# A decoder trunk on one core: one more gate/up unit ahead of the token-major key units, and a last output tile split over two PSUM banks

## The chip, the core and the metric

The kernel runs on one core of a Trainium2 chip. The metric is the device time of one execution in microseconds (us), lower is better. The engines are PE (TensorE, matmuls), DVE (VectorE), ACT (ScalarE), POOL (GpSimd) and SP (SyncE, whose queue issues nearly all transfers here). Each engine works through its own list of instructions in order, and waits on semaphores for the others.

## What is computed

The reference is a small decoder trunk with 256 tokens, width 1024 and two layers. Each layer is a half-step SwiGLU feed-forward block, a mixer, and a second half-step SwiGLU block. Layer 0 mixes by a gated short convolution, layer 1 by sparse attention. Between the layers a shared set of keys and values is built.

```python
def _swiglu(x, w_gate_up, w_down):
    a, b = jnp.split(x @ w_gate_up, 2, axis=-1)
    return (jax.nn.silu(a) * b) @ w_down

h = x
for layer in range(DEPTH):                      # DEPTH = 2, D_MODEL = 1024, D_FF = 2816, SEQ = 256
    h = h + 0.5 * _swiglu(_rmsnorm(h, ffn_norm[layer, 0]), ffn_w_gate_up[layer, 0], ffn_w_down[layer, 0])
    hn = _rmsnorm(h, mix_norm[layer])
    if layer < N_A_LAYERS:
        h = h + _short_conv(hn, conv_w_in[layer], conv_w[layer], conv_w_out[layer])
    else:
        h = h + _nsa(hn, nsa_w_qg[i], q_norm[i], nsa_w_o[i], *shared)
    h = h + 0.5 * _swiglu(_rmsnorm(h, ffn_norm[layer, 1]), ffn_w_gate_up[layer, 1], ffn_w_down[layer, 1])
    if layer == N_A_LAYERS - 1:
        shared = _shared_kv(h, kv_norm, kv_w, cmp_pos, cmp_w1, cmp_b1, cmp_w2, k_norm)
return h
```

Inside `_shared_kv`, two slots of keys and values are kept raw (they are compressed by a small network later), and four are used token by token.

## The kernel before

**Arithmetic.** Every fp32 product is made from two parts: a weight tile `raw` is loaded by SP, ACT casts it to a high part `whi` (two casts of 128x1024), and DVE subtracts that from `raw` to make the low part `wlo` (two subtractions of 128x1024). Activations have a high and a low part as well. Three products are then added in PSUM: high by high, high by low, low by high.

**Units.** The program is a list of units. A unit is one weight tile with the matmuls that use it (`mm`) and what follows them (`post`). The load of a unit's weights is issued three units ahead, its split into `whi` and `wlo` is put two units ahead (`wsplit`, `LOOK`). `at_mid(u, i, f)` hangs a piece of work `f` into unit u after its i-th step. `run_units` writes all of this as one list of operations, and `Plan.schedule` reorders it with a cost model into one fixed list per engine.

**The feed-forward block and the key units.** `ffn` makes 22 gate/up units (`gate_up(ft)`, written g0, g1, ... below), then 16 down units (`down(dt, c)`: output tile dt, half c of the inner dimension). In the third block, `between(ft)` puts the units of the shared keys and values ahead of `gate_up(ft)`, by the table `KVAT`. They are `r0`, `r1` (`rawslot`: the raw slots), `t00`, `t01`, `t10`, `t11` (`tokmajor`: keys and values token by token, two units each for one result), `c00` to `c11` (`compress`) and pieces of side work. Before the change, PE's list runs r0, g0, r1, g1, t00, t01, g2, c00, g3, c01, g4, and so on.

**PSUM.** The result of a gate/up, raw or token-major unit is a pair of banks from `two_banks()`, a pool (`psA`, tile name `pa`) with two such pairs, handed out in turn. t00 and t01 share one pair. A unit may only start when the last reader of the pair's tile before is done. The readers: after a gate/up unit ACT copies half of it (`t<-pa`) and DVE adds the other half (`t<-pa,t`); after a raw unit DVE makes eight `rt<-pa,R` multiplications. For each raw unit POOL then adds positions in two operations (`rf<-rt`), ACT casts the two results and DVE subtracts (`r<-rf`, names r00, r01, r10, r11).

**Two ways to multiply.** `halves_mm` needs two matmuls for a step of 128 rows of the inner dimension, one of 512 columns (high and low activations side by side) and one of 256, and leaves two sums in the two halves of a bank, which must be added at the end. `feature_mm` needs three matmuls of 256 columns and leaves a single sum in half a bank.

**The output.** In the last block `residual` makes each output tile from a bank with two sums: two DVE operations (`scalar_tensor_tensor`, the second reads what the first wrote) and a transfer to HBM.

Of the kernel before, what the change touches and what calls it, by code (L numbers as in the profile page):

```python
# [11 lines left out]
F32 = mybir.dt.float32  # L12
# [3 lines left out]
ALU = mybir.AluOpType  # L16
# [4 lines left out]
T = 256  # L21
DT = D // 128
NF = 2816 // 128
HALF = NF // 2
# [15 lines left out]
CQ, CO, PQ, PO = 0, 0, 4, 6  # L40
YP = 1
SB, PB, FB = 4, 4, 0
KVAT = {0: [("r0",)], 1: [("r1",)], 2: [("t00",), ("t01",)], 3: [("c00",)], 4: [("c01", (4, "k0"), (7, "k1"))],
        5: [("t10", (4, "h0")), ("t11",)], 6: [("c10", (3, "sk"), (7, "sl"))], 7: [("c11",), ("", (3, "h1"), (9, "sv"))]}
HEADP = set()
WARMUP = 9
HEAD = [("h", 0, 1), (0, 0, 2), (0, 2, 4), ("h", 1, 2), (0, 4, 8), ("h", 2, 3), (0, 8, 12), ("h", 3, 4), (0, 12, 16),
# [385 lines left out]
def program(plan, a, out, ones):  # L433
    pe, ac, ve, gp, sp = (Engine(plan, k, None) for k in ("pe", "act", "dve", "gp", "sp"))
# [4 lines left out]
    work = plan.pool("work", 2)  # L439
    psB = plan.pool("psB", 2, psum=True)  # L440
    psC = plan.pool("psC", 2, psum=True)
# [13 lines left out]
    def two_banks():  # L455
        return wide["pool"].tile([128, 2, 512], F32, name="pa")

    def tt(eng, o, x, y, op):
        eng.tensor_tensor(o, x, y, op)

    def split(hi, lo, src):
        ac.copy(hi, src)
        tt(ve, lo, src, hi.bitcast(F32), ALU.subtract)

    def mm3(o, lh, ll, rh, rl, start, stop):
        pe.matmul(o, lh, rh, start=start, stop=False)
        pe.matmul(o, lh, rl, start=False, stop=False)
        pe.matmul(o, ll, rh, start=False, stop=stop)
# [3 lines left out]
    h = px[:, NPAR:].rearrange("p (a b) -> p a b", b=T)  # L472
# [17 lines left out]
    def unit(src, n, mm, post=None):  # L490
        units.append((src, n, mm, post))
        return len(units) - 1
# [61 lines left out]
    def at_mid(u, i, f):  # L554
        mid.setdefault(u, []).append((i, f))
# [67 lines left out]
    def residual(dt, ps, factor, key, gains):  # L623
        a, b = ps[:, :T], ps[:, T:]
        if gains is None:
            o = work.tile([128, T], F32, name="s1")
            ve.scalar_tensor_tensor(o, a, factor, h[:, dt], op0=ALU.mult, op1=ALU.add)
            ve.scalar_tensor_tensor(o, b, factor, o, op0=ALU.mult, op1=ALU.add)
            sp.dma_start(out[dt * 128:(dt + 1) * 128, :], o)
            return  # L630
        if dt == 0:
            NORM[key] = new_norm(gains)
        ve.scalar_tensor_tensor(h[:, dt], a, factor, h[:, dt], op0=ALU.mult, op1=ALU.add)
        ve.scalar_tensor_tensor(h[:, dt], b, factor, h[:, dt], op0=ALU.mult, op1=ALU.add)
        norm_tile(NORM[key], dt)

    def feature_mm(ps, w, kt0, x, start, stop):

        wh, wl = w
        n = wh.shape[1] // 128  # L640
        for kt in range(n):
            s = slice(kt * 128, (kt + 1) * 128)
            mm3(ps, wh[:, s], wl[:, s], x[:, kt0 + kt, 0], x[:, kt0 + kt, 1], start and kt == 0, stop and kt == n - 1)
            yield

    def halves_mm(ps, w, kt0, x, start, stop):

        wh, wl = w
        n = wh.shape[1] // 128
        for kt in range(n):  # L650
            s = slice(kt * 128, (kt + 1) * 128)
            pe.matmul(ps, wh[:, s], x[:, kt0 + kt].rearrange("p x t -> p (x t)"), start=start and kt == 0, stop=False)
            pe.matmul(ps[:, T:], wl[:, s], x[:, kt0 + kt, 0], start=False, stop=stop and kt == n - 1)
            yield

    def halves_sum(o, x, y):
        ac.copy(o, y)
        tt(ve, o, x, o, ALU.add)


    def ffn(lf, nkey, gname, okey, ogains, pool_open, between=None):
        st = {}
        fin = {}

        def spare(ft):
            return (nkey, ft) in (("n0", 2), ("n5", 0))

        def gate_up(ft):
            paired = nkey == "n0" and ft < 2

            def mm_pair(wh, wl):
                xs = NORM[nkey].sets[gname]
                if ft == 0:
                    for i in range(2):
                        ps = two_banks()
                        st["ps", i] = [ps] + [ps[:, ab] for ab in range(2)]
                pq = [st["ps", x // 2][x % 2 - 2] for x in range(4)]
                w = [[(y[:, (4 * k + x) * 128:(4 * k + x + 1) * 128]) for y in (wh, wl)] for k in range(4) for x in range(4)]
                for k in range(4):
                    kt = 4 * ft + k  # L680
                    if kt == 0:
                        for x in range(4):
                            pe.matmul(pq[x][:, :T], w[x][0], xs[:, 0, 0], start=True, stop=False)
                        for x in range(4):
                            pe.matmul(pq[x][:, T:], w[x][1], xs[:, 0, 0], start=False, stop=False)
                        for x in range(4):
                            pe.matmul(pq[x][:, T:], w[x][0], xs[:, 0, 1], start=False, stop=False)
                            yield
                        continue
                    for x in range(4):  # L690
                        yield from halves_mm(pq[x], w[4 * k + x], kt, xs, False, kt == DT - 1)

            def mm(wh, wl):
                xs = NORM[nkey].sets[gname]
                if spare(ft):
                    ps = [psB.tile([128, 512], F32, name="pb") for _ in range(2)]
                else:
                    ps = two_banks()
                    ps = [ps] + [ps[:, ab] for ab in range(2)]
                st["ps", ft] = ps  # L700
                for kt in range(DT):
                    for ab in range(2):
                        s = slice((2 * kt + ab) * 128, (2 * kt + ab + 1) * 128)
                        yield from halves_mm(ps[ab - 2], (wh[:, s], wl[:, s]), kt, xs, kt == 0, kt == DT - 1)

            def post():
                ps = st.pop(("ps", ft))
                t = work.tile([128, 2, T], F32, name="t2")
                R = NORM[nkey].R
                if spare(ft):  # L710
                    for ab in range(2):
                        halves_sum(t[:, ab], ps[ab][:, :T], ps[ab][:, T:])
                else:
                    halves_sum(t, ps[0][:, :, :T], ps[0][:, :, T:])
                tt(ve, t, t, R[:, None, :].to_broadcast([128, 2, T]), ALU.mult)
                s = work.tile([128, T], F32, name="s1")
                ac.activation(s, t[:, 0], AF.Silu)
                g = work.tile([128, T], F32, name="g1")
                tt(gp, g, s, t[:, 1], ALU.mult)
                st["g", ft] = g  # L720

            def fin_():
                if ft % HALF == 0:
                    st["gg", ft // HALF] = pool_open(st, ft // HALF).tile([128, HALF, 2, T], F32R, name=f"gg{ft // HALF}")
                g = st["gg", ft // HALF][:, ft % HALF]
                split(g[:, 0], g[:, 1], st.pop(("g", ft)))
            if paired:
                held.append((post, fin_))
                return unit(a["wgu"][lf * NF + ft], 2048, mm_pair)
            u = unit(a["wgu"][lf * NF + ft], 2048, mm, post)  # L730
            at_mid(u + 1, 1, fin_)
            return u

        def down(dt, c):
            def mm(wh, wl):
                if c == 0:
                    st["pd"] = psB.tile([128, 512], F32, name="pb")
                yield from halves_mm(st["pd"], (wh[:, :HALF * 128], wl[:, :HALF * 128]), 0,
                                      st["gg", c], c == 0, c == 1)

            def post():
                if c == 1:
                    residual(dt, st["pd"], 0.5, okey, ogains)
            return unit(a["wdn"][lf, dt, c], HALF * 128, mm, post)

        u0 = len(units)
        for ft in range(NF):
            if between is not None:
                between(ft)
            gate_up(ft)  # L750
        for dt in range(DT):
            for c in range(2):
                down(dt, c)
        return u0
# [106 lines left out]
    def shared_kv(nkey, gname):  # L861
# [210 lines left out]
        def between(ft):  # L1072
            for name, *hooks in KVAT.get(ft, []):
                u = make[name]() if name else len(units)
# [386 lines left out]
    for u, x, y in HEAD:  # L1461
        if u == "h":
            x, y = NPAR * (x > 0) + x * T, NPAR + y * T
# [142 lines left out]
```

## Time and profile before

| | us |
|---|---|
| median of three runs (lowest, highest) | 993.74 (993.33, 993.93) |
| the profiled execution's own time | 990.6 |
| its span, from the first to the last instruction | 988.8 |
| PE busy | 978.0 (99%) |
| DVE busy | 732.6 (74%) |
| ACT busy | 584.4 (59%) |
| POOL busy | 201.6 (20%) |

The span is 1.8 us shorter than the execution, and the execution 3.1 us shorter than the median of the runs. PE is busy nearly all the time, but matmuls are pipelined, so its busy time says less than the distance from the start of one to the start of the next: in a gate/up unit a pair of 512 and 256 columns starts every 0.35 us. Small pauses of PE are spread over the attention part; in the feed-forward blocks there are few.

### The profile page before, as it was taken

How to read it: one execution, taken by the hardware profiler on the slowest of the kernel's cores; microseconds unless marked ns; L12 is line 12 of the kernel's file. 1: busy time of each engine (PE TensorE's matmuls, PEld its weight loads, DVE VectorE, ACT ScalarE, POOL GpSimd, SP SyncE). 2: the span in 40 equal slices, each digit the busy share in tenths (PEclk: the TensorE clock that was granted, in tenths of full speed). 3: DMA queues.
4: the chain of work that ended last, by engine and by line, in shares of the span. 5: the costliest groups of instructions: out<-in, count | busy, mean ns of one | idle time of the engine just before them, and what ended most of it. 6: DMA issues, size and time to landing. Idle time of an engine off the chain costs nothing.

```text
span 988.8 us, 15226 instructions
## 1 busy us (share of the span) xinstructions
PE 978.0 (99%) x5792; PEld 857.7 (87%) x5792; DVE 732.6 (74%) x1087; ACT 584.4 (59%) x1047; POOL 201.6 (20%) x263
## 2 busy tenths in 40 slices
PE   9999999999999999999999999999999999999998
PEld 6888888888888888888888888888988988888887
DVE  7876666689796767677889986666778897676553
ACT  7655645555466565555478656554599775656441
POOL 2211111122221111111340111111378421111100
PEclk9999999999999999999999999999999999999999
DMA  8655445655646454456466655355510345555353
GB/s 298 236 199 175 168 149 200 203 163 193 239 172 212 172 204 152 159 193 230 179 211 215 221 210 196 127 196 176 228 66 1 117 153 201 205 178 170 125 192 109
DMA packets 30889, 177.83 MB, mean 180 GB/s; under 512 B 3424, under 2 KB 5472, under 8 KB 15968
## 3 DMA queue, kind: packets, MB, share of 16 engines
q1 hardware_dynamic: 30816, 176.86, 52.1%
q8 instruction: 45, 0.74, 0.3%
q14 instruction: 28, 0.23, 0.1%
HBM read 175.80 MB, written 1.05 MB: 179 GB/s over the span
## 4 chain that ended last, share of the span: by engine, by line
PE 87%; ACT 5%; DVE 4%; issue 2%; DMA 1%; POOL 1%; SPq 0%; POOLq 0%; DVEq 0%; ACTq 0%
PE pa L420 53%; PE pb L420 29%; PE S L420 3%; ACT P L420 3%; PE pc L420 2%; DVE wlo L420 1%; DMA raw<-in_wgu_dram 1%; ACT ph L420 1%; DVE hg L420 1%; ACT whi L420 1%; DVE px L420 0%; DVE s L420 0%; ACT qs L420 0%; DVE r L420 0%; POOL rf L420 0%
## 5 line engine op out<-in xcount | busy, mean ns | idle before, releaser
L420 PE MATMUL pa<-hg,whi 128*128 128x512 f32 (+1 forms) x1572 | 538.4, 389 | 1.4 <-ACT whi L420 1.0
L420 DVE TENSOR_TENSOR wlo<-raw,whi 128x1024 fp32r<-128x1024 f32 (+3 forms) x382 | 415.5, 1103 | 149.6 <-ACT whi L420 147.6
L420 ACT CAST whi<-raw 128x1024 fp32r<-128x1024 f32 (+3 forms) x386 | 350.7, 931 | 204.8 <-issue 83.0
L420 PE MATMUL pa<-hg,wlo 128*128 128x256 f32 x1536 | 429.8, 280 | 0.6 <-DVE wlo L420 0.6
L420 PEld LDWEIGHTS pa<-hg,whi 128*128 128x128 f32 x1572 | 292.1, 188 | 66.0 <-ACT whi L420 2.0
L420 PEld LDWEIGHTS pa<-hg,wlo 128*128 128x128 f32 x1536 | 289.9, 189 | 2.5 <-DVE wlo L420 2.0
L420 PE MATMUL pb<-gg,whi 128*128 128x512 f32 x704 | 245.0, 393 | 0.0
L420 PE MATMUL pb<-gg,wlo 128*128 128x256 f32 x704 | 195.9, 279 | 0.0
L420 PEld LDWEIGHTS pb<-gg,whi 128*128 128x128 f32 x704 | 131.8, 187 | 30.1
L420 POOL TENSOR_TENSOR g<-s,t 128x256 f32<-128x256 f32 x88 | 70.6, 803 | 421.8 <-ACT s L420 415.7
L420 PEld LDWEIGHTS pb<-gg,wlo 128*128 128x128 f32 x704 | 132.6, 188 | 0.3
L420 ACT ACTIVATE s<-t 128x256 f32<-128x256 f32 x88 | 36.8, 418 | 130.8 <-DVE t L420 130.8
L420 POOL TENSOR_TENSOR acc<-acc,sq 128x256 f32<-128x256 f32 x36 | 32.7, 907 | 179.8 <-ACT sq L420 179.3
L420 DVE TENSOR_TENSOR t<-t,R 128x512 f32<-128x512 f32 x96 | 65.7, 685 | 0.1
L420 DVE TENSOR_TENSOR t<-pa,t 128x512 f32<-128x512 f32 x94 | 64.2, 684 | 1.8 <-ACT t L420 1.7
L420 ACT COPY t<-pa 128x512 f32<-128x512 f32 x94 | 54.1, 577 | 1.1 <-PE pa L420 1.1
L420 DVE SCALAR_TENSOR_TENSOR px<-pb,px 128x256 f32<-128x256 f32 x56 | 23.7, 424 | 34.4 <-PE pb L420 33.6
L420 PE MATMUL S<-hg,whi 128*128 128x256 f32 (+1 forms) x224 | 48.7, 301 | 0.0
L420 PE MATMUL pb<-hg,whi 128*128 128x512 f32 (+1 forms) x144 | 47.9, 384 | 0.2 <-DVE hg L420 0.2
L420 DVE TENSOR_TENSOR gg<-g,gg 128x256 fp32r<-128x256 f32 x88 | 39.2, 446 | 10.7 <-ACT gg L420 10.7
L420 ACT CAST gg<-g 128x256 fp32r<-128x256 f32 x88 | 35.3, 402 | 11.7 <-POOL g L420 11.6
L420 DVE SCALAR_TENSOR_TENSOR hg<-px,hg 128x256 fp32r<-128x256 f32 x56 | 39.3, 716 | 0.2
(178 smaller groups left out, 864.1 us busy)
## 6 DMA issues: line engine op xcount, KB each, us to landing
raw<-in_wgu_dram SPq DMA_DIRECT2D x86, 1024.0 KB, 4.8
raw<-in_wdn_dram SPq DMA_DIRECT2D x64, 704.0 KB, 4.1
raw<-in_wci_dram SPq DMA_DIRECT2D x8, 1024.0 KB, 5.0
raw<-in_wci_dram SPq DMA_DIRECT2D x8, 512.0 KB, 3.6
raw<-in_wco_dram SPq DMA_DIRECT2D x4, 1024.0 KB, 4.8
raw<-in_wkt_dram SPq DMA_DIRECT2D x4, 1024.0 KB, 4.9
raw<-in_wc_dram SPq DMA_DIRECT2D x4, 1024.0 KB, 4.8
raw<-in_wq_dram SPq DMA_DIRECT2D x4, 1024.0 KB, 4.9
```

Source lines behind the costliest of these rows:

```text
L420: getattr(engines[op.eng], op.name)(*[real(x) for x in op.args], **{k: real(v) for k, v in op.kw.items()})
```

## The change

The first part is in the table `KVAT`: from t00 on, each entry moves to the next `ft`, so that g2 comes ahead of t00 and every later key unit comes one gate/up unit later. The second is in `down`: for the last output tile of the last block (dt = 7) the two halves c = 0 and c = 1 no longer add into one bank. Half 0 goes into a bank of its own by `halves_mm`, and after it two DVE operations add it to `h`. Half 1 goes into half a bank of the pool `psC` by `feature_mm`, and one DVE operation makes the output from it and `h`.

```diff
-KVAT = {0: [("r0",)], 1: [("r1",)], 2: [("t00",), ("t01",)], 3: [("c00",)], 4: [("c01", (4, "k0"), (7, "k1"))],
-        5: [("t10", (4, "h0")), ("t11",)], 6: [("c10", (3, "sk"), (7, "sl"))], 7: [("c11",), ("", (3, "h1"), (9, "sv"))]}
+KVAT = {0: [("r0",)], 1: [("r1",)], 3: [("t00",), ("t01",)], 4: [("c00",)], 5: [("c01", (4, "k0"), (7, "k1"))],
+        6: [("t10", (4, "h0")), ("t11",)], 7: [("c10", (3, "sk"), (7, "sl"))], 8: [("c11",), ("", (3, "h1"), (9, "sv"))]}
...
         def down(dt, c):
             def mm(wh, wl):
+                if dt == DT - 1 and ogains is None:
+                    ps = (psC if c else psB).tile([128, 512], F32, name="pc" if c else "pb")
+                    st["pd", c] = ps
+                    if c == 0:
+                        yield from halves_mm(ps, (wh[:, :HALF * 128], wl[:, :HALF * 128]), 0, st["gg", c], True, True)
+                    else:
+                        yield from feature_mm(ps[:, :T], (wh[:, :HALF * 128], wl[:, :HALF * 128]), 0, st["gg", c], True, True)
+                    return
                 if c == 0:
                     st["pd"] = psB.tile([128, 512], F32, name="pb")
...
             def post():
+                if dt == DT - 1 and ogains is None:
+                    if c == 0:
+                        for x in (st["pd", 0][:, :T], st["pd", 0][:, T:]):
+                            ve.scalar_tensor_tensor(h[:, dt], x, 0.5, h[:, dt], op0=ALU.mult, op1=ALU.add)
+                        return
+                    o = work.tile([128, T], F32, name="s1")
+                    ve.scalar_tensor_tensor(o, st["pd", 1][:, :T], 0.5, h[:, dt], op0=ALU.mult, op1=ALU.add)
+                    sp.dma_start(out[dt * 128:(dt + 1) * 128, :], o)
+                    return
                 if c == 1:
                     residual(dt, st["pd"], 0.5, okey, ogains)
```

Outside the key part of the third block and the last tile, the lists of PE are the same. The first place is PE from the end of r1 on, before the change. `pa_4633` is the bank pair of r1, `pa_4715` that of g1, `pa_4775` that of t00 and t01, `pa_4852` that of g2. Weights stand on the left in t00 and t01, activations (`hg`) in the others.

```order
L420 MATMUL pa_4633<-hg_4024,wlo_4521 128x256
L420 MATMUL pa_4715<-hg_4029,whi_4596 128x512 [waits DVE_49]
...
L420 MATMUL pa_4715<-hg_4029,wlo_4617 128x256
L420 MATMUL pa_4775<-whi_4651,hg_4024 128x512 [waits DVE_49,PE_49,Activation_49]
...
L420 MATMUL pa_4775<-wlo_4740,hg_4024 128x512
L420 MATMUL pa_4775<-whi_4717,hg_4024 128x512
L420 MATMUL pa_4852<-hg_4029,whi_4778 128x512 [waits DVE_49]
```

The same stretch of PE after the change, where `pa_4775` is the pair of g2 and `pa_4824` that of t00 and t01.

```order
L420 MATMUL pa_4633<-hg_4024,wlo_4521 128x256
L420 MATMUL pa_4715<-hg_4029,whi_4596 128x512 [waits DVE_49]
...
L420 MATMUL pa_4715<-hg_4029,wlo_4617 128x256
L420 MATMUL pa_4775<-hg_4029,whi_4651 128x512 [waits DVE_49,PE_49,Activation_49]
...
L420 MATMUL pa_4775<-hg_4029,wlo_4674 128x256
L420 MATMUL pa_4824<-whi_4717,hg_4024 128x512 [waits DVE_49]
L420 MATMUL pa_4824<-wlo_4740,hg_4024 128x512
```

g2 now takes the pair that r1 had, and t00 the pair that g1 had. The second place is DVE from the readers of r1's pair on, after the change; before the change the same operations stand there in the same order, with other weights behind the names `wlo`. `t2_4787<-pa_4715` is the last reader of g1's pair, `t2_4834<-pa_4775` that of g2's.

```order
L420 TENSOR_TENSOR rt_4655<-pa_4633,R_4591 64x128 x8
L420 TENSOR_TENSOR wlo_4740<-raw_4549,whi_4717 128x1024 x2
L420 TENSOR_TENSOR gg0_4701<-g1_4686,gg0_4701 128x256
L420 TENSOR_TENSOR r10_4756<-rf0_4743,r10_4756 128x8x64
L420 TENSOR_TENSOR r11_4771<-rf1_4753,r11_4771 128x8x64
L420 TENSOR_TENSOR wlo_4790<-raw_4648,whi_4778 128x1024
L420 TENSOR_TENSOR t2_4787<-pa_4715,t2_4787 128x512
L420 TENSOR_TENSOR wlo_4790<-raw_4648,whi_4778 128x1024
L420 TENSOR_TENSOR t2_4787<-t2_4787,R_4591 128x512
L420 TENSOR_TENSOR wlo_4837<-raw_4713,whi_4826 128x1024
L420 TENSOR_TENSOR t2_4834<-pa_4775,t2_4834 128x512
```

Up to the second `wlo_4790` nothing moved on DVE; what moved is the unit on PE that these operations release. The third place is the end of DVE's list (before with -, after with +), where `s` is the output tile and `px` holds `h`.

```order
 L420 SCALAR_TENSOR_TENSOR s_9840<-pb,s_9840 128x256
 L420 TENSOR_TENSOR wlo<-raw,whi 128x704 x2
-L420 SCALAR_TENSOR_TENSOR s_9893<-pb,px 128x256
-L420 SCALAR_TENSOR_TENSOR s_9893<-pb,s_9893 128x256
+L420 SCALAR_TENSOR_TENSOR px<-pb,px 128x256 x2
+L420 SCALAR_TENSOR_TENSOR s_9907<-pc,px 128x256
```

Three operations stand where two stood, and the last one reads `pc` alone.

## Rows read from the trace of the kernel before

**Rows 1.** The page: busy time of each engine, share of the span, instructions.
```profile
PE 978.0 (99%) x5792; PEld 857.7 (87%) x5792; DVE 732.6 (74%) x1087; ACT 584.4 (59%) x1047; POOL 201.6 (20%) x263
```

**Rows 2.** The page: the chain that ended last, share of the span by engine.
```profile
PE 87%; ACT 5%; DVE 4%; issue 2%; DMA 1%; POOL 1%; SPq 0%; POOLq 0%; DVEq 0%; ACTq 0%
```

**Rows 3.** Waits of PE: waited for, us in total, times, longest us.
```profile
PE pa L420 <- DVE rt L420: 1.1, 1, 1.1
```

**Rows 4.** Timeline of PE, end of g1 and start of t00: start us, us, operation.
```profile
491.74 0.28 PE L420 MATMUL pa<-hg,wlo 128*128 128x256 f32 x1
493.07 0.47 PE L420 MATMUL pa<-whi,hg 128*128 128x512 f32 x1 [1.05 <-DVE rt L420]
```

**Rows 5.** PE by stretch (r1, g1, t00+t01, g2): us, busy (matmuls), granted clock, DMA.
```profile
480.46:486.21 5.75, 5.75 (x51) 1.00 0.35 118
486.21:491.86 5.65, 5.65 (x34) 1.00 0.36 126
493.07:504.07 11.00, 10.99 (x48) 1.00 0.33 114
504.07:509.71 5.64, 5.64 (x33) 1.00 0.66 225
```

**Rows 6.** Timeline of DVE from the readers of r1's pair to g1's.
```profile
490.52 2.41 DVE L420 TENSOR_TENSOR rt<-pa,R 64x128 f32<-64x128 f32 x8
492.96 3.51 DVE L420 TENSOR_TENSOR wlo<-raw,whi 128x1024 fp32r<-128x1024 f32 x2
...
497.86 2.25 DVE L420 TENSOR_TENSOR r<-rf,r 128x512 fp32r<-128x512 f32 x2
500.04 1.21 DVE L420 TENSOR_TENSOR wlo<-raw,whi 128x1024 fp32r<-128x1024 f32 x1
501.27 0.69 DVE L420 TENSOR_TENSOR t<-pa,t 128x512 f32<-128x512 f32 x1
```

**Rows 7.** Timeline of ACT in the same stretch.
```profile
497.68 1.35 ACT L420 CAST r<-rf 128x512 fp32r<-128x512 f32 x2 [0.94 <-POOL rf L420]
498.94 1.04 ACT L420 CAST whi<-raw 128x1024 fp32r<-128x1024 f32 x1
499.89 0.57 ACT L420 COPY t<-pa 128x512 f32<-128x512 f32 x1
```

**Rows 8.** Timeline of POOL in the same stretch.
```profile
493.10 4.55 POOL L420 TENSOR_TENSOR rf<-rt,kvc 128x528 f32<-128x528 f32 x2 [4.71 <-DVE rt L420]
```

**Rows 9.** Timeline of PE at the start of the span.
```profile
0.77 3.76 PE L420 MATMUL pc<-const-bfloat16-1.0 128*128 128x512 bf16 x9 [0.77 <-PEq L1596]
4.18 0.58 PE L420 MATMUL pa<-hg,whi 128*128 128x256 f32 x2
```

**Rows 10.** All engines at the end: us, PE, PEld, DVE, ACT, POOL busy, granted clock, DMA.
```profile
985.20:987.10 1.90, 0.00 (x0) 0.00 (x0) 0.85 (x2) 0.00 (x0) 0.00 (x0) 1.00 0.05 17
987.20:988.80 1.60, 0.00 (x0) 0.00 (x0) 0.00 (x0) 0.00 (x0) 0.00 (x0) 0.50 0.12 41
```

**Rows 11.** Timeline: ACT's last read of t00's pair, and PE's start of g3 there.
```profile
508.30 0.68 ACT L420 ACTIVATE kk<-pa,nr 128x512 f32<-128x512 f32 x1
...
511.61 0.39 PE L420 MATMUL pa<-hg,whi 128*128 128x512 f32 x1
```

**Rows 12.** Timeline of the last down unit and of what follows it.
```profile
981.21 0.40 PE L420 MATMUL pb<-gg,whi 128*128 128x512 f32 x1
...
984.91 0.28 PE L420 MATMUL pb<-gg,wlo 128*128 128x256 f32 x1
985.23 0.42 DVE L420 SCALAR_TENSOR_TENSOR s<-pb,px 128x256 f32<-128x256 f32 x1 [5.14 <-PE pb L420]
985.69 0.42 DVE L420 SCALAR_TENSOR_TENSOR s<-pb,s 128x256 f32<-128x256 f32 x1
986.14 0.34 SPq L420 DMA_DIRECT2D out_dram<-s  x1
```

## The prediction

> **What bounds the kernel now.** I read the page first. PE is busy for 978.0 of 988.8 us [rows 1], and the chain that ended last runs through PE for 87% of the span [rows 2]. So an edit pays or costs by what it does to the starts of PE's matmuls, and by what it does after the last one. Then I read PE's waits. In the key part there is one of more than a microsecond, and it is DVE's `rt` that ends it [rows 3]. The timeline of PE shows the place: the last matmul of g1 starts at 491.74 and the first of t00 at 493.07, with 1.05 us of idle time before it [rows 4]. A look at DVE says why. t00 takes the bank pair of r1, and the eight `rt` operations that read r1's result stand in DVE's list behind other work, so they end only at 490.52 + 2.41 = 492.93 [rows 6]; PE starts 0.14 us later. Last I read the tail: after the last matmul there are two DVE operations and one transfer [rows 12].
>
> **Step 1: the wait that the change is placed at.** With g2 ahead of t00, PE's next unit after g1 is g2. The pairs are handed out in turn, so g2 takes r1's pair, exactly as t00 did. DVE's list is the same up to that point, and what stands ahead of `rt` on DVE hangs on ACT and POOL work that is the same too; the load of g2's weights comes ahead of those of t00 on SP's queue, but each is 1 MB and is issued at the same points. So `rt` still ends at 492.93, and g2 starts where t00 started, at 493.07. This wait is not removed; it only has another unit behind it. Gain: 0.
>
> **Step 2: a new wait in front of t00.** g2 takes 5.64 us [rows 5], so it is done at 493.07 + 5.64 = 498.71. Then PE wants t00, which now takes the pair of g1. Its last reader is DVE's `t<-pa,t` for g1. In the kernel before, that operation ran from 501.27 and ended at 501.96 [rows 6]. There it hurt nobody, because t00 and t01 used the other pair until 504.07 [rows 5]. Its time is set by a chain that the change leaves as it is. POOL's two `rf` operations start when `rt` is done and end at 493.10 + 4.55 = 497.65 [rows 8]. ACT's casts of r11 wait for them, from 497.68 on, and behind them in ACT's list stand half a weight cast and then g1's copy, from 499.89 to 500.46 [rows 7]. On DVE the subtractions for r10 and r11 (497.86 to 500.11) and half a weight split (500.04 to 501.25) stand ahead of `t<-pa,t` [rows 6]. While POOL runs `rf`, DVE is slower as well: a weight split of two halves took 3.51 us at 492.96, against 2 x 1.21 for the half at 500.04 [rows 6, 8]. None of these operations is passed by another in the new lists. So t00 starts at 501.96 + 0.14 = 502.10, and PE stands still for 502.10 - 498.71 = 3.4 us. Then t00 and t01 take 11.00 us [rows 5] and end at 513.10, where the kernel before had the same three units done at 509.71: **+3.4 us**. Behind the waiting matmul stands the rest of PE's list. ACT, DVE and SP wait for that in turn, as they are fed by buffers that PE's units give back. Bounds: the chain may vary by some 0.2 us either way (the idle time of ACT before r11's casts alone is 0.94 us, so a slower ACT is absorbed and a slower POOL isn't).
>
> **Step 3: what comes later in the key part.** All later key units keep their distance in units, and each has at least the slack that it had. One example: g3 takes the pair of t00 before the change. ACT's last read of that pair ended at 508.30 + 0.68 = 508.98 and g3 started at 511.61, 2.6 us later [rows 11]; after the change it is g4 that takes this pair, 7.5 us after t01 instead of 1.9. I cost this at nothing; the cover is the gate/up units between. The last key unit comes one gate/up unit later, still 13 units ahead of the down units.
>
> **Step 4: the clock.** A pause of 3.4 us is longer than any inside this kernel. What the rows show: in the stretch after the 1.05 us pause the granted clock was 1.00, which is 2.4 GHz [rows 5]. At the end of the span PE stops after its matmul of 984.91 [rows 12]; the granted clock was still 1.00 until 987.10 and was 0.50, which is 1.2 GHz, from 987.20 on [rows 10]. So a stop of about 2 us was followed by a fall, and one of 1 us was not. 3.4 us lies beyond the first, so I take it that the clock falls. The price: at the start the nine warm-up matmuls of 512 columns came every (3.76 - 0.39) / 8 = 0.42 us, and after 3.4 us of them, at 4.18, the real work began [rows 9]; t00 and t01 show 11.00 / 48 = 0.229 us for 512 columns at 2.4 GHz [rows 5]. If t00 runs at 1.2 GHz for as long as PE did at the start, 3.4 us, it does the work of 1.7 us: **+1.7 us**. Bounds: 0 (no fall) and 2.1 (half of the 4.18 us from the span's start to that first real matmul).
>
> The Trainium skill, "TensorE: Matmul & The Clock Gate", section "HAM oscillation — how this bites in real kernels", says that a wait for data between groups of matmuls can put the array back to half rate, so that the next group begins cold. By that rule the sum has the 1.7 us in it; without it the sum is 1.7 us smaller. The fall to 0.50 at the end of the span agrees; that it happens in the middle of work, no row here shows.
>
> **Step 5: the tail.** Before: the last matmul starts at 984.91, DVE's two operations start at 985.23 and 985.69, and SP issues the transfer at 986.14 [rows 12]. After: the sums of half 0 are added to `h` while half 1 runs. That is 2 x 0.42 us on an engine that stood idle for 5.14 us there [rows 12]: nothing on the path. One operation is left, so 985.69 - 985.23 = 0.46 us go. Against that, half 1 has three matmuls of 256 columns a step instead of 512 + 256. r1 has this form, 16 steps in 5.75 us, and g1 beside it the other, 16 steps in 5.65 [rows 5]: 0.006 us more a step. The last unit itself is faster than g1: 11 steps from 981.21 to 985.02, 0.346 a step, against 0.359 in r1, 0.013 more. 11 steps cost 0.07 to 0.14; I take 0.10. **Net -0.36 us**, with bounds -0.46 and 0 (the last operation reads PSUM where its twin read PSUM too, so I see no loss).
>
> The same page of the Trainium skill, section "Back-to-back issue gap", gives a fixed 2.5 ns a matmul beyond its columns; by it 11 more matmuls cost 0.03 us (an estimate), and the tail would be -0.43. The rows show more, 0.07 to 0.14, and they are used.
>
> **The sum.** 0 + 3.4 + 0 + 1.7 - 0.36 = +4.74 us. The profiled span goes from 988.8 to 993.5 and its execution from 990.6 to 995.3. The median of the runs lies 3.14 us above the profiled execution, so 993.74 + 4.74 = **998.5 us**.
>
> **The rivals.**
> A, the forecast: the new wait and a fall of the clock, 998.5.
> B: the new wait, but the clock stays up. For it: a stop of this length in the middle of work is not in the trace, and at the end 2 us passed before the fall. The rest of the sum stays: 993.74 + 3.4 - 0.36 = 996.8.
> C, not slower: g1's pair is free before g2 ends. The place is DVE's `t<-pa,t`; the point is that it must end before 498.6, which is 3.4 us earlier than in this trace. That needs ACT's copy of g1 ahead of the casts of r10 and r11 and DVE's half likewise. If so, nothing waits at t00, and the time is 993.74 - 0.36 = 993.4; if r1's wait went too (-1.05), it is 992.3. Against it: the new lists keep the order, and POOL's 4.55 us stand ahead of them.
> D: the pause costs more, because work that stood in PE's shadow comes due late in the key part, or the clock stays down for longer: another 1 to 3 us, 999.5 to 1001.5. For it I see no row.
>
> **How the numbers follow.** A 0.66, B 0.19, C 0.09, D 0.06. The likeliest is A, 998.5. The range is to hold A and B: its lower end is B with the wait 0.2 shorter and the tail at its best, 993.74 + 3.2 - 0.46 = 996.5, rounded to 996.4; its upper end is A with the wait 0.2 longer, 2.1 for the clock and no gain in the tail, 993.74 + 3.6 + 2.1 = 999.4. Faster or slower by over 0.2% means by over 2 us, about what a measurement of this kernel can tell from no change. A, B and D are slower by more than that: 0.91. C is mostly within it, 0.06, and 0.03 is left for faster.
>
> **What would show it.** Step 1: an idle time of about 1 us before g2's first matmul, ended by DVE's `rt`. Step 2: one of about 3.4 us before t00's first matmul (the first with weights on the left, `pa<-whi,hg`), ended by DVE's `t`, near 502.1. Step 4: a granted clock below 1.00 in the next few microseconds, with 512 columns every 0.42 us. Step 5: one DVE operation between the last matmul and the last transfer, and the end of the span some 3.0 us (no fall) or 4.7 us later than 988.8. I am wrong if t00 follows g2 without a pause, or if the pause is there and the time did not rise.

## The result: slower by half a per cent

The changed kernel takes 998.25 us (median of 4 runs, 996.83 to 999.19) where the kernel before takes 993.74: a ratio of 1.0052, 95% interval 1.0032 to 1.0072, or +5.2 us with +3.2 to +7.2. The forecast was 998.5, case A. A second comparison of the same two kernels gave 997.22 against 992.66 (1.0039, 1.0024 to 1.0054).

Waits of PE in the changed kernel, in the columns of [rows 3]:

```profile
PE pa L420 <- DVE t L420: 3.2, 1, 3.2
...
PE pa L420 <- DVE rt L420: 1.0, 1, 1.0
```

The old wait for `rt` is still there, and a new one, three times as long, stands above it. The timeline of PE shows the two places, as [rows 4] did for one: end of g1 and start of g2, end of g2 and start of t00.

```profile
492.23 0.28 PE L420 MATMUL pa<-hg,wlo 128*128 128x256 f32 x1
493.54 0.47 PE L420 MATMUL pa<-hg,whi 128*128 128x512 f32 x1 [1.03 <-DVE rt L420]
...
499.05 0.28 PE L420 MATMUL pa<-hg,wlo 128*128 128x256 f32 x1
502.52 0.79 PE L420 MATMUL pa<-whi,hg 128*128 128x512 f32 x1 [3.19 <-DVE t L420]
503.11 0.63 PE L420 MATMUL pa<-wlo,hg 128*128 128x512 f32 x1
```

In the row that waits for `rt` the activations (`hg`) stand on the left, so it is g2; in the row that waits for `t` the weights do, so it is t00. From one matmul to the next it is 0.43 us after that (503.11 to 503.54), not 0.23. DVE's timeline in this stretch, which answers to [rows 6]:

```profile
493.43 3.51 DVE L420 TENSOR_TENSOR wlo<-raw,whi 128x1024 fp32r<-128x1024 f32 x2
496.86 1.54 DVE L420 TENSOR_TENSOR gg<-g,gg 128x256 fp32r<-128x256 f32 x1
498.33 2.21 DVE L420 TENSOR_TENSOR r<-rf,r 128x512 fp32r<-128x512 f32 x2
500.51 1.23 DVE L420 TENSOR_TENSOR wlo<-raw,whi 128x1024 fp32r<-128x1024 f32 x1
501.77 0.69 DVE L420 TENSOR_TENSOR t<-pa,t 128x512 f32<-128x512 f32 x1
```

POOL's and ACT's, which answer to [rows 7, 8]:

```profile
493.57 4.55 POOL L420 TENSOR_TENSOR rf<-rt,kvc 128x528 f32<-128x528 f32 x2 [4.68 <-DVE rt L420]
```

```profile
498.15 1.38 ACT L420 CAST r<-rf 128x512 fp32r<-128x512 f32 x2 [0.90 <-POOL rf L420]
499.44 1.04 ACT L420 CAST whi<-raw 128x1024 fp32r<-128x1024 f32 x1
500.39 0.57 ACT L420 COPY t<-pa 128x512 f32<-128x512 f32 x1
```

Each operation that [rows 6 to 8] show has its place and, to 0.04 us, its length of before, all of it 0.5 us later because this execution reached the key part 0.5 us later. The last reader of g1's pair ends at 501.77 + 0.69 = 502.46, and t00 starts 0.06 us after that. The clock of PE around the pause, by stretch (columns: us, PE busy and matmuls, granted clock, DMA share, GB/s):

```profile
499.40:501.20 1.80, 0.00 (x0) 1.00 0.92 387
501.30:502.50 1.20, 0.00 (x0) 0.50 0.00 0
502.60:508.00 5.40, 5.40 (x13) 0.50 0.59 194
508.10:516.10 8.00, 8.00 (x36) 1.00 0.46 147
```

The clock fell to 0.50, which is 1.2 GHz, while PE stood still, and PE then worked at that level until 508.0, 5.5 us. t00 and t01 took 13.63 us instead of 11.00. The end of the program, the rows that answer to [rows 12]: first matmul of the last unit's second half, DVE's one addition, SP's transfer.

```profile
990.14 0.40 PE L420 MATMUL pc<-gg,whi 128*128 128x256 f32 x2
...
994.29 0.42 DVE L420 SCALAR_TENSOR_TENSOR s<-pc,px 128x256 f32<-128x256 f32 x1 [3.06 <-PE pc L420]
994.74 0.34 SPq L420 DMA_DIRECT2D out_dram<-s  x1
```

From the first matmul of the last half to the transfer it is 994.74 - 990.14 = 4.60 us; it was 986.14 - 981.21 = 4.93 [rows 12].

**How to compare two profiles here.** The two profiled spans differ by 8.6 us, the medians by 4.5: the profiled execution of before (990.6) was faster than its three timed runs shown ahead of the prediction, and that of after (999.19) is the slowest of its four. So I cut the span into pieces that can be read in any of these kernels: from the span's start to the end of r0, from there to the first matmul of c00 (less 5.65 us for each gate/up unit more, [rows 5]), from there to the last matmul (with these 5.65 us added back), and the rest. The mark at the end of r0 is the first of its last two matmuls on `whi`; r0 itself begins 7.93 us earlier in each of these profiles, and PE's list mixes its steps with those of g0. All times are starts of matmuls in PE's timeline, in us; the rows from "keys part alone" on are the experiments.

| kernel | end of r0 | from there to c00, less added units | against before | c00 to last matmul, with them |
|---|---|---|---|---|
| before | 476.43 | 33.28 | | 475.19 |
| after | 476.92 | 39.22 | +5.94 | 477.83 |
| before, again | 479.32 | 33.31 | +0.03 | 475.23 |
| after, again | 477.19 | 38.22 | +4.94 | 476.39 |
| keys part alone | 477.02 | 38.19 | +4.91 | 477.66 |
| tail alone | 477.48 | 33.23 | -0.05 | 477.67 |
| two units more | 477.35 | 38.21 | +4.93 | 475.57 |
| pause filled | 477.01 | 36.66 | +3.38 | 477.06 |
| one rf on DVE | 474.77 | 35.00 | +1.72 | 475.45 |
| g2 in other banks | 474.74 | 31.96 | -1.32 | 477.83 |
| the same, again | 478.12 | 31.96 | -1.32 | 475.48 |
| g1 in other banks, old order | 476.67 | 32.01 | -1.27 | 476.27 |
| the same, again | 477.07 | 32.01 | -1.27 | 477.64 |

The middle column is the change's own stretch, and it repeats to 0.05 us for one kernel, but for the first profile of after, whose extra 1.0 us is a longer stretch of low clock (below). The outer columns move by 4.6 and 2.6 us between executions, also where PE's list is word for word the same (474.74 and 478.12 for one kernel). That is the noise behind every median here. For the same reason the absolute times in the expectations, which start from 993.74 and 998.25, are read as differences below: in the comparisons with the experiments the kernel before came out at 991.35, 992.66 and 992.70.

### The profile page after: what moved, and what is told of

The parts are those of the page before. It is cut to its first block, busy times and chain, and to the rows that moved or that the text cites. A ratio compares the mean times of both kernels' runs of the same rounds, so it can differ in the third digit from the quotient of the medians.

```text
span 997.4 us, 15247 instructions
## 1 busy us (share of the span) xinstructions
PE 984.1 (99%) x5803; PEld 860.7 (86%) x5803; DVE 731.9 (73%) x1088; ACT 585.5 (59%) x1047; POOL 202.4 (20%) x263
## 3 DMA queue, kind: packets, MB, share of 16 engines
HBM read 175.80 MB, written 1.05 MB: 177 GB/s over the span
## 4 chain that ended last, share of the span: by engine, by line
PE 88%; ACT 5%; DVE 4%; issue 2%; POOL 1%; DMA 0%; SPq 0%; POOLq 0%; ACTq 0%
PE pa L420 53%; PE pb L420 29%; PE S L420 3%; PE pc L420 3%; ACT P L420 2%; DVE wlo L420 1%; ACT ph L420 1%; ACT whi L420 1%; DVE hg L420 1%; DVE px L420 0%; DMA raw<-in_wgu_dram 0%; POOL P L420 0%; DVE r L420 0%; DVE s L420 0%; ACT qs L420 0%
## 5 line engine op out<-in xcount | busy, mean ns | idle before, releaser
L420 PE MATMUL pb<-gg,whi 128*128 128x512 f32 x693 | 242.2, 395 | 0.0
L420 PE MATMUL pb<-gg,wlo 128*128 128x256 f32 x693 | 192.9, 279 | 0.0
L420 PEld LDWEIGHTS pb<-gg,wlo 128*128 128x128 f32 x693 | 130.5, 188 | 0.3
```

The source lines that it names most:

```text
L420: getattr(engines[op.eng], op.name)(*[real(x) for x in op.args], **{k: real(v) for k, v in op.kw.items()})
```

## The experiments

T1 is the prediction's theory: the time goes to the hand-over of g1's bank pair and to the clock that falls in that pause, and the tail gives a little back. The rivals: R1, the later place of the key units costs by itself; R2, the clock is the whole loss; R3, the tail costs.

**Each half of the change alone.** First the table of the key part, with the old tail (the edit is the hunk on `KVAT` alone).

```diff
-KVAT = {0: [("r0",)], 1: [("r1",)], 2: [("t00",), ("t01",)], ...
+KVAT = {0: [("r0",)], 1: [("r1",)], 3: [("t00",), ("t01",)], ...
```

> The changed kernel with the old tail: the last output tile in one bank and two additions. T1 (the loss is the wait of t00 for g1's bank pair, 3.4 us, and a fall of the clock): the pause of about 3.2 to 3.4 us before t00 is there, the clock falls after it, and the time is 998.25 + 0.36 = 998.6 us, between 997 and 999.6. R3 (the new tail costs, it does not gain): the time is below that of the changed kernel, 997.9 or less.

Measured: 997.31 against 991.35 (1.0063, 1.0049 to 1.0078), +6.2 us with +4.9 to +7.7. The wait is there, on `t`:

```profile
502.60 0.50 PE L420 MATMUL pa<-whi,hg 128*128 128x512 f32 x1 [3.07 <-DVE t L420]
```

t00 and t01 took 515.22 - 502.60 = 12.62 us. So the key part carries the whole loss. The 997.31 lies under R3's mark of 997.9 only because the kernel before was 2.4 us faster in this comparison; as a difference it is no smaller than the changed kernel's +5.2, so R3 gets no support. Then the tail alone, `KVAT` as before:

```diff
 def post():
+    if dt == DT - 1 and ogains is None:
+        ...
     if c == 1:
         residual(dt, st["pd"], 0.5, okey, ogains)
```

> The kernel before with the new tail alone: the order of the key part is the old one, t00 behind g1. T1 and the step on the tail: one addition of 0.42 us fewer after the last matmul, 0.10 us more of matmuls, so 993.74 - 0.36 = 993.4 us, and the wait of 1.05 us before t00 is there as before. R3 (the tail costs): 993.9 or more. R1 (the two-bank tail also shifts work in the last block): a change of more than 1 us either way.

Measured: 991.66 against 991.35 (1.0003, 0.9993 to 1.0013), so between -0.7 and +1.3 us: a gain of a third of a microsecond can't be told from nothing by these times. The trace shows it, though: the first matmul of the last half starts at 984.56 and the transfer at 989.16, which is 4.60 us, as in the changed kernel, and 0.33 less than before.

```profile
984.56 0.40 PE L420 MATMUL pc<-gg,whi 128*128 128x256 f32 x2
...
989.16 0.34 SPq L420 DMA_DIRECT2D out_dram<-s  x1
```

**Whose bank, and is the unit more worth anything?** In the changed kernel g2 is put into two banks of the other pool, which nobody uses at that point. No unit changes its place on PE, but t00 now gets r1's pair; what reads g2's result is done bank by bank, in two copies and two additions instead of one of each.

```diff
 def spare(ft):
-    return (nkey, ft) in (("n0", 2), ("n5", 0))
+    return (nkey, ft) in (("n0", 2), ("n3", 2), ("n5", 0))
```

> The changed kernel, but g2 writes its two halves into two banks of the other pool (pb), which stand idle in the key part. So t00 takes r1's pair and g3 takes g1's. T1 (bank hand-over is the cause): no wait of 1.03 us at g2 and none of 3.2 us at t00, the clock stays at 1.00 through t00 and t01, and the time is 993.74 - 1.05 - 0.36 = 992.3 us (991.8 to 993.0), below both kernels. R1 (the later place of the key part itself costs, by work that comes due late or by slower gate/up units in the fourth block): the pause is gone but the time stays 2 us or more above that, 994.3 to 995.5. R2 (the clock alone): as T1 at t00, since there is no pause to let it fall.

Measured: 990.38 against 991.35 (0.9984, 0.9972 to 0.9996). Start of g2 and of t00 in PE's timeline:

```profile
490.05 0.28 PE L420 MATMUL pa<-hg,wlo 128*128 128x256 f32 x1
490.17 0.40 PE L420 MATMUL pb<-hg,whi 128*128 128x512 f32 x1
...
495.71 0.28 PE L420 MATMUL pb<-hg,wlo 128*128 128x256 f32 x1
495.83 0.40 PE L420 MATMUL pa<-whi,hg 128*128 128x512 f32 x1
```

Each follows the matmul ahead of it by 0.12 us, where the changed kernel stood still for 1.03 and 3.19. The inputs of both units are there in time; it was only the banks that were not. This speaks against R1 as well: the key units stand just as late as in the changed kernel, and the stretch from the end of r0 to c00 is 1.32 us shorter than before.

The twin of it leaves the order as it was, has the new tail, and puts g1 there, so that t00 takes g0's pair.

```diff
-    return (nkey, ft) in (("n0", 2), ("n5", 0))
+    return (nkey, ft) in (("n0", 2), ("n3", 1), ("n5", 0))
```

> The kernel before with the new tail, its key part in the old order, but g1 writes its halves into two banks of the other pool (pb), so that t00 takes g0's pair and no longer r1's. T1: the wait of 1.05 us before t00 goes and no other comes, so 1.05 to 1.3 for the wait and 0.33 for the tail: 1.4 to 1.6 us below before, the same as with g2 in the other banks. Rival (the extra unit between the raw and the token-major keys has a worth of its own, once no bank is waited for): this kernel is slower than the one with g2 in the other banks by 1 us or more, with a new wait in the key part.

Measured: 989.70 against 992.66 (0.9969, 0.9952 to 0.9987), and 1.27 us less from the end of r0 to c00. The two were then run once more, side by side.

> The old order with g1 in two banks of the other pool and the new tail, once more, beside the kernel with g2 there. T1: 1.4 to 1.6 us below before (0.9985), and the same as its neighbour within 1 us. Rival (the unit more has a worth or a price of its own): the two differ by more than 1 us.

> The changed kernel with g2 in two banks of the other pool, once more, beside the kernel with g1 there. T1: 1.4 to 1.6 us below before, no wait of over 1 us in the key part. Rival: as for its neighbour.

Measured: 990.24 (0.9981, 0.9967 to 0.9995) for g1 and 989.68 (0.9976, 0.9964 to 0.9988) for g2, both against 992.70. They are the fastest versions of this study, and 0.56 us apart, with 32.01 and 31.96 us from the end of r0 to c00. So a gate/up unit between the raw and the token-major keys is worth nothing in itself that these runs can tell; the two kernels gain because neither waits for a bank. About 1.3 + 0.33 = 1.6 us of their gain is shown by the traces, and all four intervals hold that (as -0.4 to -2.8 us for the first, from 0.9996 and 0.9972). Medians beyond it, down to -3.0, can't be told from the spread of executions.

**Wait or clock?** 14 matmuls of 512 columns on constants, whose result nobody reads, are put between g2 and t00, so that PE works where it stood still.

```diff
+def fill(n):
+    t = psC.tile([128, 512], F32, name="pc")
+    ...
+        op = pe.matmul(t, ones[:, :128], ones, start=True, stop=True)
```

> The changed kernel, with 14 matmuls of 512 columns on constants added between g2 and t00; they write a bank that nobody reads, so the output is the same and only PE's idle time is filled. 14 x 0.215 = 3.0 us of the 3.2 us pause. T1 (wait and clock are two terms): t00 still starts when DVE's t for g1 is done, the clock stays at 1.00 through t00, and the time is 998.25 less the clock's share: 1.7 to 2.8 us less, 995.5 to 996.6. B-like rival (the clock costs nothing here): 998.3 and a clock that falls all the same. R2 (the clock is the whole loss): 993.5 to 994.

Measured: 993.81 against 991.35 (1.0032, 1.0019 to 1.0045), +3.2 us. The filler and t00 by stretch:

```profile
499.55:502.60 3.05, 3.01 (x13) 1.00 0.53 223
502.67:513.60 10.93, 10.93 (x48) 1.00 0.57 193
```

t00 starts at 502.67, as late as ever, so the wait itself is 3.4 us of the loss; but the clock stays at 1.00, and t00 and t01 take 11.02 us again. R2 is out: its mark of 993.5 to 994 stood for no loss at all, and against the kernel before in the same comparison +3.2 us are left, with +1.9 at the low end of the interval. So is the idea that the clock is free: the 1.6 us between this kernel's +3.38 and the +4.9 of the others is the clock.

**The same, later.** Two gate/up units more instead of one.

```diff
-KVAT = {0: [("r0",)], 1: [("r1",)], 3: [("t00",), ("t01",)], 4: [("c00",)], ...
+KVAT = {0: [("r0",)], 1: [("r1",)], 4: [("t00",), ("t01",)], 5: [("c00",)], ...
```

> The changed kernel with two more gate/up units between the raw key units and the token-major ones instead of one: r0, g0, r1, g1, g2, g3, t00. T1 (the wait belongs to the bank pair of g1, whoever takes it next): it is now g3 that takes it, so PE stands still for 3.2 to 3.4 us before g3's first matmul (a gate/up unit, activations on the left), t00 starts without a wait, the clock falls in g3, and the time is that of the changed kernel, 5 to 6 us above before. Rival (t00's own inputs or weights come late): no pause at g3, one of what is left at t00; with 5.65 us more behind g2 nothing is left, and the time is 0.3 below to 0.5 above before.

Measured: 998.00 against 992.66 (1.0047, 1.0030 to 1.0064). PE at g2, g3 and t00:

```profile
494.01 0.47 PE L420 MATMUL pa<-hg,whi 128*128 128x512 f32 x1 [1.07 <-DVE rt L420]
...
503.00 0.63 PE L420 MATMUL pa<-hg,whi 128*128 128x512 f32 x1 [3.21 <-DVE t L420]
...
510.17 0.28 PE L420 MATMUL pa<-hg,wlo 128*128 128x256 f32 x1
510.28 0.40 PE L420 MATMUL pa<-whi,hg 128*128 128x512 f32 x1
```

The pause has moved to a gate/up unit, with the same length and the same releaser, and t00 starts without one. Whichever unit comes second behind g1 pays for g1's pair.

**What holds the pair.** The second `rf` addition for r1 goes from POOL to DVE. With it the order on ACT and DVE changes: the cast and the subtraction of r11 now stand behind the two readers of g1's pair.

```diff
-tt(gp, f.rearrange("p (a b) -> p a b", b=8),
+tt(ve if s and hh else gp, f.rearrange("p (a b) -> p a b", b=8),
```

> The changed kernel with the second of r1's two rf additions on DVE instead of POOL. POOL's part of the chain behind the wait of t00 shrinks from 4.55 us to about 2.3, and in ACT's and DVE's lists the cast and the subtraction of r11 now stand behind the copy and the addition that read g1's pair. T1 (step 2: that chain sets when g1's pair is free): POOL ends near 495.9, DVE's t ends near 500.5 instead of 502.46, the wait at t00 is 1 to 2 us instead of 3.2, and if so short a pause leaves the clock at 1.00, the time is 3.4 to 4.5 us below the changed kernel: 0.5 to 2 us above before. If the clock falls all the same: 2 us below the changed kernel. Rival (something else holds the pair, as the load or the split of the weights): the wait stays at 3.2 us and the time at 5 us above before.

Measured: 992.91 against 992.70 (1.0012, 0.9998 to 1.0027), which is +1.2 us with -0.2 to +2.7 and so some 3 to 4 us below the changed kernel (+5.2 and +3.9); from the end of r0 to c00 it is 4.94 - 1.72 = 3.2 us. POOL, then DVE, then PE:

```profile
491.43 2.29 POOL L420 TENSOR_TENSOR rf<-rt,kvc 128x528 f32<-128x528 f32 x1 [4.69 <-DVE rt L420]
...
492.43 2.36 DVE L420 TENSOR_TENSOR wlo<-raw,whi 128x1024 fp32r<-128x1024 f32 x1
...
496.77 1.22 DVE L420 TENSOR_TENSOR wlo<-raw,whi 128x1024 fp32r<-128x1024 f32 x1
498.03 0.69 DVE L420 TENSOR_TENSOR t<-pa,t 128x512 f32<-128x512 f32 x1
...
498.77 0.50 PE L420 MATMUL pa<-whi,hg 128*128 128x512 f32 x1 [1.58 <-DVE t L420]
```

The wait is 1.58 us, half of what it was, and so short a pause left the clock alone:

```profile
497.20:498.70 1.50, 0.00 (x0) 1.00 1.03 437
498.77:509.70 10.93, 10.93 (x48) 1.00 0.56 197
```

So it is the chain of step 2 that sets when g1's pair is free. How much of the halving is POOL's 2.26 us and how much the new place of r11 was not told apart.

**The two kernels again, unchanged.**

> The kernel before, unchanged, in another execution. It measures how far executions of one program differ. In the profile of before the gate/up units of the last block ran with 230 ns between matmuls of 512 columns; in the changed kernel and in all four kernels tried so far two thirds of them ran at 241 ns, which is 2.2 us. If this varies from execution to execution, the new profile may show it here too, and the time is 991.35 with a spread of 990.0 to 993.8 as its other runs. If it belongs to the changes (R1: any change of the list shifts work in the last block), this profile shows 230 ns again and the same 2.2 us advantage.

Measured: 992.61 against 992.66 of its other runs in the same comparison. The question was about the gate/up units of the last block, where the first profile of after had fewer matmuls in 100 us than that of before. Stretches of 100 us of PE in gate/up units, with the count of matmuls in brackets; first the second block, in the first profile of before and in its second:

```profile
300.00:400.00 100.00, 100.00 (x579) 1.00 0.52 180
```

```profile
300.00:400.00 100.00, 100.00 (x569) 1.00 0.52 179
```

Then the last block, in the first profile of after and in its second:

```profile
820.00:920.00 100.00, 100.00 (x568) 1.00 0.53 183
```

```profile
820.00:920.00 100.00, 100.00 (x578) 1.00 0.56 188
```

The starts do lie farther apart: from a matmul of 512 columns to the next one it is 0.236 us on average in the two stretches with fewer, 0.230 in the others. Ten matmuls of 579 fewer are about 2 us over such a block, and either kernel has one execution with the slower pace and one without. So the pace belongs to an execution and not to a kernel, and nothing here speaks for R1; why the pace changes, no run here tells.

> The changed kernel, unchanged, in another execution. T1: the pause before t00 again 3.2 to 3.5 us, ended by DVE's t; the granted clock falls again, either for 3.4 us (as with the keys part alone, where t00 and t01 took 12.6 us) or for 6.8 us (as in the first profile, 13.6 us). Time against before: 1.005 to 1.006, the same within the interval as the first result.

Measured: 997.22 against 992.66, the pause again 3.18 us, ended by `t`, and the clock by stretch:

```profile
499.70:502.70 3.00, 0.00 (x0) 1.00 0.54 227
503.20:506.50 3.30, 3.30 (x9) 0.50 0.50 122
506.60:515.40 8.80, 8.80 (x40) 1.00 0.62 202
```

Here it fell only after t00 had begun, and t00 and t01 took 12.60 us.

## Why the prediction was right, step by step

**Step 1** (the wait of 1.05 us stays, in front of g2) held: 1.03 us, ended by `rt`.

**Step 2** (t00 waits 3.4 us for g1's pair) held in place, cause and size. The idle time is 3.1 to 3.2 us in all four profiles with the pause; counted as the prediction did, from 5.64 us after g2's start, it is 502.52 - 499.18 = 3.34. The filled kernel, which has the wait without the clock, is 3.38 us longer from the end of r0 to c00. Other banks take the pause away, another unit in t00's place inherits it, and a shorter chain halves it.

**Step 3** (nothing later) held as far as it can be seen. Its example has one distance wrong, without harm: before the change g3 already started 511.61 - 504.07 = 7.5 us after t00 and t01 were done [rows 5, 11], not 1.9, and after it g4 does so 523.69 - 516.15 = 7.5 us after them. The slack stayed as it was; it didn't grow. The stretch from c00 to the last matmul was 475.2 to 477.8 us in all kernels; those with later key units stand at both ends (475.45, 475.48 and 475.57; 477.66 and 477.83), and so do those without (475.19; 477.64 and 477.67).

**Step 4** (the clock falls, +1.7, bounds 0 and 2.1) held in sign, and in size in three profiles of four: with PE at 0.50 for 3.3 us, these kernels lost 4.9 - 3.38 = 1.6 us beyond the wait. In the fourth, the first profile of after, PE worked at 0.50 for 5.5 us and lost 2.63, more than the upper bound. The step that failed there is "for as long as PE did at the start": that was one sample of how long the low clock lasts, taken as its length. That execution took 999.19 us and is what rival D allowed for, a clock that stays down for longer. The Trainium skill, "TensorE: Matmul & The Clock Gate", section "HAM oscillation — how this bites in real kernels", on which one sentence of the prediction leant, says that a wait for data between groups of matmuls can make the next group start cold; the four profiles with the pause agree, and the filled one shows that it is the idle time that does it.

**Step 5** (the tail, -0.36) held in the trace, -0.33: one addition of 0.46 us less, 0.13 more for matmuls. The timed run of the tail alone can't confirm it.

**The sum** was +4.74, and the two comparisons gave +4.5 and +4.6 between medians. By the traces it is 4.94 - 0.33 = 4.6 us in the second profile of the changed kernel and 5.94 - 0.33 = 5.6 in the first. The sum is sound, then, but it is luck that the medians agree with it so closely, since the median of the kernel before alone moved by 2.4 us between comparisons (993.74 and 991.35). Rival C stood at the right place: where no bank is waited for, the kernel is not slower. But that took other banks, which the change doesn't have.

## What to carry over

A unit that is put ahead of a waiting one doesn't fill the wait if both draw their banks from one ring: it takes the bank that the other waited for, and pushes the other onto the next bank, whose readers may be later still. So list the bank of each unit and the end of its last reader, before and after, and price each pair by that. A pause that brings the clock down costs more than itself; here 3.2 us cost 4.9 and in one execution 5.9, while after pauses of 1.0 and 1.6 us the clock stayed up.

## What the runs showed of the hardware

- After a pause of 3.1 to 3.2 us the granted clock was at 0.50 for 3.3 us of PE's work in three executions and for 5.5 in one; in that one it had fallen inside the pause. After pauses of 1.0 and 1.6 us it stayed at 1.00.
- DVE and POOL hold each other up. In the kernel with one `rf` on DVE, POOL's `rf` ran from 491.43 to 493.72. The half weight split that DVE had begun before it, at 491.29, took its usual 1.23 us; the next, begun at 492.43, took 2.36, that is 1.14 more, and ended 1.07 us after POOL did. POOL is slower beside DVE as well: in the kernel before, `g<-s,t` of 128x256 took 0.73 to 0.75 us in the 65 of 88 cases in which nothing ran on DVE beside it, and up to 1.49 in the others. The Trainium skill, "SBUF — State Buffer", section "SBUF: two separate sides", describes a port pair that whichever of the two starts first holds for its whole instruction while the other blocks; these rows agree. So POOL's 4.55 us in step 2's chain may hold waits for DVE, as DVE's splits hold waits for POOL; no run here has the additions on POOL alone. The page's busy times don't show it: the one that waits counts as busy meanwhile.
- PE's matmuls of the gate/up units run at two paces, 579 or about 569 in 100 us, at a granted clock of 1.00 in both, and the same stretch of a kernel can have one pace in one execution and the other in another.
